# Two output rows share one middle-tap product in a dilated 3x3 convolution, with deeper f32 prefetch and two-bank PSUM tiles

## The chip, the cores and the metric

The kernel runs on one core of one Trainium2 chip; nothing else runs on the chip. The metric is the device time of one execution in microseconds (us). The *span* that a profile shows runs from the first to the last instruction and is about 2 us shorter than the time. All kernels here were timed in several rounds beside the kernel before. A difference under 2% counts as the same.

## The reference

A 3x3 convolution with dilation 2 and padding 2, f32 in and out:

```python
batch, c_in, h, w, c_out, k, dilation = 16, 64, 64, 64, 128, 3, 2
x_pad = np.pad(x, ((0, 0), (0, 0), (2, 2), (2, 2)))
output[b, co] += weight[co, ci, kh, kw] * x_pad[b, ci, kh*2 : kh*2+h, kw*2 : kw*2+w]   # summed over ci, kh, kw
```

The input is 16.8 MB, the output 33.6 MB. An output row r needs the input rows r-2, r and r+2, so rows of one parity of a pair never mix with the other parity.

## The kernel before

Two images share the 128 partitions (64 input channels each). Each is multiplied by its own 64-row half of the TensorE array, so the matmuls of the two images run side by side. A tile is 8 rows of one image: nine matmuls of up to 512 columns, one for each tap (one of the nine weights of the 3x3 window), are summed in one bank of PSUM, the memory into which TensorE writes here. Then the bank is copied to SBUF, from which DMA stores it.

```python
x32pool = ctx.enter_context(tc.tile_pool(name="x32pool", bufs=2))     # a whole pair of images, f32
cpool = ctx.enter_context(tc.tile_pool(name="cpsum", bufs=8, space=bass.MemoryType.PSUM))
# ... zero-padded f16 rows of 68 columns, weights transposed by TensorE: cut ...
def conv_matmul(x3, ps, ti, t, hb, first, last):
    dh, dw = taps[t]
    # ... rows clipped at the image's edge: cut ...
    rhs = x3[hb * CI : (hb + 1) * CI, lo + dh : hi + dh, pad + dw : pad + dw + W]
    nc.tensor.matmul(out=po, lhsT=lhsT, rhs=rhs, start=first, stop=last)

for pb in range(npairs):                      # 8 pairs of images
    for ti in range(ntiles):                  # 8 tiles of 8 rows
        for t in range(ntaps):                # 9 taps
            for hb in range(2):
                conv_matmul(x3, ps, ti, t, hb, t == 0, t == ntaps - 1)
        # ... loads and f32 -> f16 casts of the next pair: cut ...
        nc.vector.tensor_copy(out=o_sb0[:, sl], in_=ps[0])    # the engines swap on odd tiles
        nc.scalar.copy(out=o_sb1[:, sl], in_=ps[1])
        # stores of 1 MB, in the last pair of 256 KB after each tile: cut
```

## Time and profile before

| | before |
|---|---|
| time, median of 4 runs beside the change | 142.72 us (142.18 to 143.32) |
| span of the profiled run | 140.7 us |
| TensorE busy | 125.1 us |
| first to last convolution matmul | 10.6 to 134.2 us, no gap |
| bytes moved | 50.66 MB |
| DMA rate from 30 to 80 us | 423 GB/s |

Two limits lie within 3% of each other. The page of the kernel before gives, first, the busy time of each engine with its share of the span, then the span in 40 slices of 3.5 us: a digit is the busy share in tenths, and the last line is the rate of DMA. PE stands for TensorE's matmuls, PEld for its weight loads, DVE for VectorE, ACT for ScalarE, POOL for GpSimd and SP for SyncE; L133 is line 133 of the kernel.

```profile
PE 125.1 (89%) x1170; PEld 71.5 (51%) x1170; DVE 55.7 (40%) x85; ACT 53.8 (38%) x86; POOL 21.4 (15%) x49
...
PE   0049999999999999999999999999999999999910
...
DMA  4999999999999999999999999892929385799970
GB/s 97 296 415 418 415 401 414 344 428 418 424 422 422 428 417 425 429 411 424 425 424 423 422 421 428 354 414 121 426 100 431 165 356 245 298 395 402 388 307 8
```

Counted from 0, TensorE's row is full from slice 3 to slice 37. DMA's row is full only from slice 1 to slice 24, and from then on it has holes. The table by stages of the same kernel shows this in numbers. Its columns are: the stretch in us and its length, then for each engine the busy us and the number of instructions, the granted clock, the busy share of DMA and its rate.

```profile
core 0: us, PE busy (x) PEld busy (x) DVE busy (x) ACT busy (x) POOL busy (x), PEclk, DMA share, GB/s
0.00:5.00 5.00, 0.00 (x0) 0.00 (x0) 0.40 (x1) 1.28 (x1) 2.31 (x13) 1.00 0.57 136
...
30.00:80.00 50.00, 50.00 (x476) 28.58 (x473) 22.46 (x33) 20.58 (x33) 6.32 (x12) 1.00 1.02 423
...
90.00:100.00 10.00, 10.00 (x96) 5.61 (x93) 3.46 (x5) 3.09 (x6) 1.36 (x3) 1.00 0.74 308
100.00:110.00 10.00, 10.00 (x99) 5.80 (x96) 4.15 (x6) 3.35 (x6) 1.05 (x2) 1.00 0.75 312
110.00:120.00 10.00, 10.00 (x100) 5.77 (x96) 3.46 (x5) 2.93 (x6) 1.37 (x3) 1.00 0.56 229
...
125.00:135.00 10.00, 9.15 (x87) 4.94 (x81) 3.60 (x6) 3.15 (x6) 2.78 (x6) 1.00 0.98 382
135.00:140.70 5.70, 0.00 (x0) 0.00 (x0) 0.00 (x0) 0.00 (x0) 0.46 (x1) 0.63 0.30 119
```

From 30 to 80 us DMA moves 423 GB/s with a busy share of 1.02, so it is saturated; all 50.66 MB at that rate are 120 us. From 90 to 120 us the rate falls to 229 to 312 GB/s. All loads are done by then, and stores come only as fast as TensorE makes output. TensorE is busy in all of these stretches. So DMA has slack, and TensorE sets the end. The timeline of TensorE near the end gives its pace (start, duration, instruction):

```profile
128.14 0.38 PE L133 MATMUL ps_1593<-x_sb_81,w_sb 64*128 64x512 f16 x1
128.33 0.38 PE L133 MATMUL ps_1594<-x_sb_81,w_sb 64*128 64x512 f16 x1
...
130.08 0.38 PE L133 MATMUL ps_1617<-x_sb_81,w_sb 64*128 64x512 f16 x1
```

The first matmul of one tile is at 128.14 us, that of the next at 130.08: 1.94 us for nine pairs of matmuls, 0.216 us a pair. (A matmul's own 0.38 us is longer because matmuls overlap: the first two lines start 0.19 us apart.) The costs of the other engines come from the groups of instructions, one line for one shape; the columns at the end are busy us and mean ns:

```profile
L181 DVE COPY o_sb_708<-ps_829 128x512 f32<-128x512 f32 x1 | 0.7, 692 | 1.4 <-PE ps_829 L133 1.4
```

```profile
L102 ACT CAST x_sb_84<-x_964 128x1024 f16<-128x1024 f32 x1 | 1.0, 1045 | 0.9 <-PE ps_614 L133 0.9
...
L178 ACT COPY o_sb_132<-ps_134 128x512 f32<-128x512 f32 x1 | 0.6, 585 | 0.2 <-PE ps_134 L133 0.2
```

A copy of 512 columns out of PSUM takes VectorE 0.692 us and ScalarE 0.585 us, and a cast of 1024 columns takes ScalarE 1.045 us.

### The profile page before, as it was taken

What the parts mean: (1) busy time and instruction counts of PE and PEld (TensorE: products, weight loads), DVE (VectorE), ACT (ScalarE), POOL (GpSimd) and SP (SyncE); (2) the same over time, 40 slices, a digit from 0 to 9 for tenths busy, and PEclk for the clock granted to TensorE, in tenths of its full rate; (3) what the DMA queues carried; (4) which work ended last, traced back from release to release, by engine and by line L of the source; (5) the groups of instructions that cost most, each with busy time, mean ns of one, the idle gap of its engine ahead of it and who ended that gap; (6) DMA issues with size and microseconds to landing.
All of it is one profiled execution on the core that took longest, in us unless ns stands there. A gap on an engine that the chain in (4) does not pass through costs nothing.

```text
span 140.7 us, 2777 instructions
## 1 busy us (share of the span) xinstructions
PE 125.1 (89%) x1170; PEld 71.5 (51%) x1170; DVE 55.7 (40%) x85; ACT 53.8 (38%) x86; POOL 21.4 (15%) x49
## 2 busy tenths in 40 slices
PE   0049999999999999999999999999999999999910
PEld 0035555655555555655565555555565556555500
DVE  0134556535353534445353435333233333323310
ACT  3144465652535343533635253532233333322310
POOL 6000003020202020201102030202020110433210
PEclk9999999999999999999999999999999999999985
DMA  4999999999999999999999999892929385799970
GB/s 97 296 415 418 415 401 414 344 428 418 424 422 422 428 417 425 429 411 424 425 424 423 422 421 428 354 414 121 426 100 431 165 356 245 298 395 402 388 307 8
DMA packets 10733, 50.66 MB, mean 360 GB/s; under 512 B 1248, under 2 KB 1376, under 8 KB 7136
## 3 DMA queue, kind: packets, MB, share of 16 engines
q0 software_dynamic: 4816, 31.61, 54.3%
q1 hardware_dynamic: 5904, 18.88, 34.6%
q8 instruction: 9, 0.15, 0.4%
q14 instruction: 4, 0.03, 0.1%
HBM read 17.07 MB, written 33.55 MB: 360 GB/s over the span
## 4 chain that ended last, share of the span: by engine, by line
PE 73%; issue 12%; DMA 5%; POOL 3%; SPq 1%; ACT 1%; POOLq 0%
DMA x_87<-in_x_dram 5%; POOL out_dram L185 3%; PE ps_134 L133 1%; PE ps_1378 L133 1%; PE ps_1327 L133 1%; PE ps_1235 L133 1%; PE ps_1163 L133 1%; PE ps_1114 L133 1%; PE ps_1020 L133 1%; PE ps_972 L133 1%; PE ps_923 L133 1%; PE ps_829 L133 1%; PE ps_781 L133 1%; PE ps_732 L133 1%; PE ps_638 L133 1%
## 5 line engine op out<-in xcount | busy, mean ns | idle before, releaser
L133 PEld LDWEIGHTS <-w_sb 64*128 64x128 f16 x1152 | 70.2, 94 | 53.1 <-issue 1.1
L113 PE MATMUL wt_95<-ident,w_70 128*64 128x128 f16 x1 | 0.4, 377 | 7.7 <-DMA w_70<-in_weight_dram 7.7
L185 POOL DMA_DIRECT2D out_dram<-o_sb_1471 x8 | 4.3, 541 | 10.4 <-DVE o_sb_1471 L177 5.3
L100 DVE CAST x_sb_78<-x_87 128x640 f16<-128x640 f32 (+2 forms) x3 | 1.8, 606 | 8.9 <-DMA x_87<-in_x_dram 8.9
L113 PEld LDWEIGHTS <-w_70 128*64 128x64 f16 x9 | 1.1, 209 | 7.7 <-DMA w_70<-in_weight_dram 7.7
L185 POOL DMA_DIRECT2D out_dram<-o_sb_131 x2 | 1.1, 548 | 23.1 <-ACT o_sb_131 L180 19.3
L102 ACT CAST x_sb_78<-x_87 128x512 f16<-128x512 f32 (+1 forms) x2 | 1.7, 830 | 6.4 <-DMA x_87<-in_x_dram 6.4
L133 PE MATMUL ps_133<-x_sb_78,w_sb 64*128 64x512 f16 (+1 forms) x9 | 3.4, 557 | 0.0
L133 PE MATMUL ps_134<-x_sb_78,w_sb 64*128 64x512 f16 (+1 forms) x9 | 3.2, 528 | 0.0
L185 POOL DMA_DIRECT2D out_dram<-o_sb_898 x2 | 1.1, 532 | 13.1 <-ACT o_sb_898 L180 13.1
L185 POOL DMA_DIRECT2D out_dram<-o_sb_516 x2 | 1.1, 531 | 13.1 <-ACT o_sb_516 L180 13.1
L185 POOL DMA_DIRECT2D out_dram<-o_sb_707 x2 | 1.1, 531 | 13.1 <-ACT o_sb_707 L180 13.1
L185 POOL DMA_DIRECT2D out_dram<-o_sb_1089 x2 | 1.1, 531 | 13.1 <-ACT o_sb_1089 L180 13.1
L185 POOL DMA_DIRECT2D out_dram<-o_sb_325 x2 | 1.1, 531 | 13.1 <-DVE o_sb_326 L181 13.1
L185 POOL DMA_DIRECT2D out_dram<-o_sb_1280 x2 | 1.1, 531 | 12.8 <-ACT o_sb_1280 L180 12.8
L102 ACT CAST x_sb_84<-x_391 128x1024 f16<-128x1024 f32 (+1 forms) x2 | 2.0, 992 | 2.6 <-DMA x_391<-in_x_dram 2.6
L102 ACT CAST x_sb_81<-x_200 128x1024 f16<-128x1024 f32 (+1 forms) x2 | 2.0, 990 | 2.6 <-DMA x_200<-in_x_dram 2.6
L102 ACT CAST x_sb_78<-x_582 128x1024 f16<-128x1024 f32 (+1 forms) x2 | 2.0, 994 | 1.4 <-PE ps_255 L133 1.4
L100 DVE CAST x_sb_84<-x_391 128x1152 f16<-128x1152 f32 (+1 forms) x2 | 1.5, 727 | 2.4 <-DMA x_391<-in_x_dram 2.4
L102 ACT CAST x_sb_81<-x_773 128x1024 f16<-128x1024 f32 (+1 forms) x2 | 2.0, 993 | 0.9 <-PE ps_423 L133 0.9
L102 ACT CAST x_sb_78<-x_1155 128x1024 f16<-128x1024 f32 (+1 forms) x2 | 2.0, 994 | 0.9 <-PE ps_805 L133 0.9
L102 ACT CAST x_sb_81<-x_1346 128x1024 f16<-128x1024 f32 (+1 forms) x2 | 2.0, 994 | 0.9 <-PE ps_996 L133 0.9
(309 smaller groups left out, 373.2 us busy)
## 6 DMA issues: line engine op xcount, KB each, us to landing
out_dram<-o_sb_131 POOLq DMA_DIRECT2D x2, 1024.0 KB, 10.3
out_dram<-o_sb_132 POOLq DMA_DIRECT2D x2, 1024.0 KB, 13.0
out_dram<-o_sb_325 POOLq DMA_DIRECT2D x2, 1024.0 KB, 11.1
out_dram<-o_sb_326 POOLq DMA_DIRECT2D x2, 1024.0 KB, 14.3
out_dram<-o_sb_516 POOLq DMA_DIRECT2D x2, 1024.0 KB, 11.1
out_dram<-o_sb_517 POOLq DMA_DIRECT2D x2, 1024.0 KB, 14.4
out_dram<-o_sb_707 POOLq DMA_DIRECT2D x2, 1024.0 KB, 10.8
out_dram<-o_sb_708 POOLq DMA_DIRECT2D x2, 1024.0 KB, 13.4
```

Source lines behind the costliest of these rows:

```text
L100: nc.vector.tensor_copy(out=x3[:, lo:hi, pad : pad + W], in_=x32[:, lo:hi, :])
L102: nc.scalar.copy(out=x3[:, lo:hi, pad : pad + W], in_=x32[:, lo:hi, :])
L113: nc.tensor.matmul(out=wt_ps[0:CI, 0:CO], lhsT=w_slice, rhs=ident)
L133: nc.tensor.matmul(out=po, lhsT=lhsT, rhs=rhs, start=first, stop=last)
L185: nc.gpsimd.dma_start(out=out_img[2 * pb, :, e0:e1], in_=o_sb0[:, e0:e1])
```

## The change

The intent is to take matmuls off TensorE. Take two output rows of one parity, r and r+2. With w0, w1, w2 the weights of the three rows of taps, and x the input rows:

- row r is w0 x[r-2] + w1 x[r] + w2 x[r+2]
- row r+2 is w0 x[r] + w1 x[r+2] + w2 x[r+4]

Let P = w1 (x[r] + x[r+2]). Then row r = P + (w2-w1) x[r+2] + w0 x[r-2], and row r+2 = P + (w0-w1) x[r] + w2 x[r+4]. That is five products for two rows instead of six. The price: a row sum of the input on VectorE, a copy of P out of PSUM on ScalarE, and two additions of P on VectorE in place of two plain copies. A group is now 16 rows of two images, 1024 output columns for each of P, A (the even blocks) and B (the odd ones).

```diff
-    x32pool = ctx.enter_context(tc.tile_pool(name="x32pool", bufs=2))       # whole pairs
-    cpool = ctx.enter_context(tc.tile_pool(name="cpsum", bufs=8, space=bass.MemoryType.PSUM))
+    LOOK = 6
+    XB = 8
+    x32pool = ctx.enter_context(tc.tile_pool(name="x32pool", bufs=XB))      # quarters of a pair
+    xpool = ctx.enter_context(tc.tile_pool(name="xpool", bufs=3))
+    ppool = ctx.enter_context(tc.tile_pool(name="ppool", bufs=1, space=bass.MemoryType.PSUM))
+    apool = ctx.enter_context(tc.tile_pool(name="apool", bufs=3, space=bass.MemoryType.PSUM))
     # ... weights now loaded as f32 on ScalarE's queue, w2-w1 and w0-w1 formed on VectorE: cut ...
+    def product(ps, src, kind, blk0, nblk, first, last):
+        for j in (1, 0, 2):                                  # middle column first: it covers all 64
+            dw = (j - 1) * d
+            o0, o1 = max(0, -dw), W - max(0, dw)             # clipped columns: 62 of 64 for j = 0, 2
+            # ... for hb in range(2): one matmul: cut ...
     for G in range(ngroups):                                 # 32 groups
         # ... tiles, views and z (1 at an image's edge, else 0): cut ...
+        product(psP, sv, 0, 0, NBLK, True, True)
+        product(psA, blocks(x16, b0, NBLK, 1), 1, 0, NBLK, True, False)
+        product(psA, blocks(x16, b0 + z - 1, NBLK - z, 1), 2, z, NBLK - z, False, True)
+        product(psB, blocks(x16, b0, NBLK, 0), 3, 0, NBLK, True, False)
+        product(psB, blocks(x16, b0 + 1, NBLK - z, 0), 4, 0, NBLK - z, False, True)
+        nc.scalar.copy(out=p_sb, in_=psP)
+        for e, ps in ((0, psA), (1, psB)):
+            nc.vector.tensor_tensor(out=o[:, :, b0 : b0 + NBLK, e], in0=ps..., in1=pv, op=add)
+        c = G + LAG                                          # LAG = LOOK
+        if c < ngroups:
+            cast(c)
+            rowsum(c)
+            if c + XB < ngroups:
+                load(c + XB)
     # ... two stores of 1 MB from GpSimd's queue after every second group: cut ...
```

The framework's scheduler decides the order of the instructions on each engine from these dependencies; it need not be the order of the source.

More of the change, by code (lines that the diff above doesn't have):

```diff
@@ L22 @@
     CO, CI_w, KH, KW = weight.shape
-    assert CI == CI_w
-    d = 2 if isinstance(dilation, bass.AP) else int(dilation)
-    assert KH == KW == 3
-    assert CI == 64 and CO == 128
+    assert CI == CI_w == 64 and CO == 128
+    assert KH == KW == 3 and H == W == 64
     assert B % 2 == 0
+    assert not isinstance(dilation, bass.AP) and int(dilation) == 2
+    d = 2
     P = 128
-    pad = d
-    WP = W + 2 * pad
-    HW = H * W
     f32 = mybir.dt.float32
     f16 = mybir.dt.float16
-    ROWS = 512 // W
@@ L38 @@
-    ntiles = H // ROWS
-    assert H % ROWS == 0
-    NB = ROWS * W
-    CR = 2 * ROWS
-    nchunks = ntiles // 2
-    chunk_rows = [(0, CR + d)]
-    for c in range(1, nchunks - 1):
-        chunk_rows.append((c * CR + d, (c + 1) * CR + d))
-    chunk_rows.append(((nchunks - 1) * CR + d, H))
-    assert nchunks == 4
-    chunk_rows0 = [(0, ROWS + d), (ROWS + d, CR + d)] + chunk_rows[1:]
-    taps = [(0, 0)]
-    for kh in range(KH):
-        for kw in range(KW):
-            dh = (kh - KH // 2) * d
-            dw = (kw - KW // 2) * d
-            if (dh, dw) != (0, 0):
-                taps.append((dh, dw))
@@ L58 @@
-    ntaps = len(taps)
+    add = mybir.AluOpType.add
+    sub = mybir.AluOpType.subtract
+    HW = H * W
+    GR = 16
+    NG = H // GR
+    NBLK = GR // 4
+    NH = GR // 2 * W
     npairs = B // 2
-    NXB = 3
+    ngroups = npairs * NG
+    chunk_rows = [(g * GR + (d if g else 0), min((g + 1) * GR + d, H)) for g in range(NG)]
+    LOOK = 6
+    XB = 8
     wpool = ctx.enter_context(tc.tile_pool(name="wpool", bufs=1))
-    x32pool = ctx.enter_context(tc.tile_pool(name="x32pool", bufs=2))
-    xpool = ctx.enter_context(tc.tile_pool(name="xpool", bufs=1))
@@ L66 @@
-    opool = ctx.enter_context(tc.tile_pool(name="opool", bufs=4))
-    cpool = ctx.enter_context(tc.tile_pool(name="cpsum", bufs=8, space=bass.MemoryType.PSUM))
-    w16 = wpool.tile([CO, CI * KH * KW], f16, name="w16")
-    nc.gpsimd.dma_start(out=w16, in_=weight.rearrange("o i h w -> o (i h w)"))
-    ident = wpool.tile([P, P], f16, name="ident")
-    make_identity(nc, ident)
-    w_sb = wpool.tile([P, ntaps * CO], f16, name="w_sb")
-    x3_bufs = []
-    for i in range(NXB):
-        x_sb = xpool.tile([P, H * WP], f16, tag=f"xsb{i}", name=f"x_sb{i}")
-        x3 = x_sb.rearrange("p (h w) -> p h w", w=WP)
-        nc.gpsimd.memset(x3[:, :, 0:pad], 0.0)
-        nc.gpsimd.memset(x3[:, :, pad + W :], 0.0)
-        x3_bufs.append(x3)
+    x32pool = ctx.enter_context(tc.tile_pool(name="x32pool", bufs=XB))
@@ L85 @@
+    xpool = ctx.enter_context(tc.tile_pool(name="xpool", bufs=3))
+    opool = ctx.enter_context(tc.tile_pool(name="opool", bufs=3))
+    spool = ctx.enter_context(tc.tile_pool(name="spool", bufs=3))
+    ppool = ctx.enter_context(tc.tile_pool(name="ppool", bufs=1, space=bass.MemoryType.PSUM))
+    apool = ctx.enter_context(tc.tile_pool(name="apool", bufs=3, space=bass.MemoryType.PSUM))
     x_pair = x.rearrange("(nb two) c h w -> nb (two c) h w", two=2)
@@ L88 @@
     x32_tiles = {}
-    def emit_input_dma(pb):
-        x32 = x32pool.tile([P, H, W], f32, tag="x32")
-        x32_tiles[pb] = x32
-        for lo, hi in (chunk_rows0 if pb == 0 else chunk_rows):
-            nc.sync.dma_start(out=x32[:, lo:hi], in_=x_pair[pb, :, lo:hi])
-    def emit_cast(pb, lo, hi, engine):
-        x3 = x3_bufs[pb % NXB]
-        x32 = x32_tiles[pb]
-        if engine == "v":
-            nc.vector.tensor_copy(out=x3[:, lo:hi, pad : pad + W], in_=x32[:, lo:hi, :])
-        else:
-            nc.scalar.copy(out=x3[:, lo:hi, pad : pad + W], in_=x32[:, lo:hi, :])
@@ L104 @@
-    emit_input_dma(0)
-    emit_cast(0, chunk_rows0[0][0], chunk_rows0[0][1], "v")
-    emit_cast(0, chunk_rows0[1][0], chunk_rows0[1][1], "s")
-    for t, (dh, dw) in enumerate(taps):
-        kh = dh // d + KH // 2
-        kw = dw // d + KW // 2
-        w_slice = w16.rearrange("o (i k) -> o i k", k=KH * KW)[:, :, kh * KW + kw]
-        wt_ps = cpool.tile([CO, NB], f32, tag="ps", name=f"wt{t}")
-        nc.tensor.matmul(out=wt_ps[0:CI, 0:CO], lhsT=w_slice, rhs=ident)
-        nc.tensor.matmul(out=wt_ps[CI : 2 * CI, 0:CO], lhsT=w_slice, rhs=ident)
-        dst = w_sb[:, t * CO : (t + 1) * CO]
-        if t % 2 == 0:
-            nc.scalar.copy(out=dst, in_=wt_ps[:, 0:CO])
-        else:
-            nc.vector.tensor_copy(out=dst, in_=wt_ps[:, 0:CO])
@@ L121, in conv_matmul @@
-    def conv_matmul(x3, ps, ti, t, hb, first, last):
-        dh, dw = taps[t]
-        r0 = ti * ROWS
-        lo = max(r0, -dh)
-        hi = min(r0 + ROWS, H - dh)
-        lhsT = w_sb[hb * CI : (hb + 1) * CI, t * CO : (t + 1) * CO]
-        rhs = x3[
-            hb * CI : (hb + 1) * CI,
-            lo + dh : hi + dh,
-            pad + dw : pad + dw + W,
-        ]
-        po = ps[hb][:, (lo - r0) * W : (hi - r0) * W]
-        nc.tensor.matmul(out=po, lhsT=lhsT, rhs=rhs, start=first, stop=last)
@@ L135 @@
-    for pb in range(npairs):
-        x3 = x3_bufs[pb % NXB]
-        o_sb0 = opool.tile([P, HW], f32, tag="osb")
-        o_sb1 = opool.tile([P, HW], f32, tag="osb")
-        first_pair = pb == 0
-        last_pair = pb == npairs - 1
-        if last_pair:
-            flush_after = {ti: (ti * NB, (ti + 1) * NB) for ti in range(ntiles)}
-        else:
-            flush_after = {
-                ntiles // 2 - 1: (0, HW // 2),
-                ntiles - 1: (HW // 2, HW),
-            }
-        for ti in range(ntiles):
-            ps = [
-                cpool.tile([CO, NB], f32, tag="ps", name=f"ps{hb}") for hb in range(2)
-            ]
-            for t in range(ntaps):
-                for hb in range(2):
-                    conv_matmul(x3, ps, ti, t, hb, t == 0, t == ntaps - 1)
-            if first_pair:
-                if ti == 0:
-                    emit_cast(0, chunk_rows[1][0], chunk_rows[1][1], "v")
-                    emit_cast(0, chunk_rows[2][0], chunk_rows[2][1], "s")
-                elif ti == 1:
-                    emit_cast(0, chunk_rows[3][0], chunk_rows[3][1], "v")
-            if pb + 1 < npairs:
-                if ti == 2:
-                    emit_input_dma(pb + 1)
-                elif ti == 4:
-                    emit_cast(pb + 1, chunk_rows[0][0], chunk_rows[0][1], "v")
-                    emit_cast(pb + 1, chunk_rows[1][0], chunk_rows[1][1], "s")
-                elif ti == 5:
-                    emit_cast(pb + 1, chunk_rows[2][0], chunk_rows[2][1], "v")
-                    emit_cast(pb + 1, chunk_rows[3][0], chunk_rows[3][1], "s")
-            sl = slice(ti * NB, (ti + 1) * NB)
-            if ti % 2 == 0:
-                nc.vector.tensor_copy(out=o_sb0[:, sl], in_=ps[0])
-                nc.scalar.copy(out=o_sb1[:, sl], in_=ps[1])
-            else:
-                nc.scalar.copy(out=o_sb0[:, sl], in_=ps[0])
-                nc.vector.tensor_copy(out=o_sb1[:, sl], in_=ps[1])
-            if ti in flush_after:
-                e0, e1 = flush_after[ti]
-                nc.gpsimd.dma_start(out=out_img[2 * pb, :, e0:e1], in_=o_sb0[:, e0:e1])
-                if last_pair:
-                    nc.sync.dma_start(
-                        out=out_img[2 * pb + 1, :, e0:e1], in_=o_sb1[:, e0:e1]
-                    )
-                else:
-                    nc.gpsimd.dma_start(
-                        out=out_img[2 * pb + 1, :, e0:e1], in_=o_sb1[:, e0:e1]
-                    )
@@ new lines, with load, cast @@
+    x16_tiles = {}
+    xs_tiles = {}
+    def load(c):
+        pb, g = divmod(c, NG)
+        lo, hi = chunk_rows[g]
+        t = x32pool.tile([P, (GR + d) * W], f32, tag="x32", name="x32")
+        x32_tiles[c] = t
+        nc.sync.dma_start(
+            out=t[:, 0 : (hi - lo) * W].rearrange("p (h w) -> p h w", w=W),
+            in_=x_pair[pb, :, lo:hi],
+        )
+    def cast(c):
+        pb, g = divmod(c, NG)
+        lo, hi = chunk_rows[g]
+        if g == 0:
+            x16_tiles[pb] = xpool.tile([P, HW], f16, tag="x16", name="x16")
+            xs_tiles[pb] = xpool.tile([P, HW // 2], f16, tag="xs", name="xs")
+        nc.scalar.copy(
+            out=x16_tiles[pb][:, lo * W : hi * W], in_=x32_tiles.pop(c)[:, 0 : (hi - lo) * W]
+        )
@@ new lines, in rowsum @@
+    def rowsum(c):
+        pb, g = divmod(c, NG)
+        v = x16_tiles[pb][:, g * GR * W : (g + 1) * GR * W].rearrange(
+            "p (b e q) -> p b e q", e=2, q=2 * W
+        )
+        s = xs_tiles[pb][:, g * NH : (g + 1) * NH].rearrange("p (b q) -> p b q", q=2 * W)
+        nc.vector.tensor_tensor(out=s, in0=v[:, :, 0], in1=v[:, :, 1], op=add)
+    w32 = wpool.tile([CO, CI * KH * KW], f32, name="w32")
+    nc.scalar.dma_start(out=w32, in_=weight.rearrange("o i h w -> o (i h w)"))
+    for c in range(XB):
+        if c < ngroups:
+            load(c)
@@ new lines @@
+    ident = wpool.tile([P, P], f16, name="ident")
+    make_identity(nc, ident)
+    KINDS = 5
+    wd = wpool.tile([CO, KINDS * KW * 2 * CI], f16, name="wd")
+    wdv = wd.rearrange("o (k j r i) -> o k j r i", k=KINDS, j=KW, r=2)
+    wv = w32.rearrange("o (i h w) -> o h w i", h=KH, w=KW)
+    for r in range(2):
+        nc.vector.tensor_copy(out=wdv[:, 0, :, r], in_=wv[:, 1])
+        nc.vector.tensor_tensor(out=wdv[:, 1, :, r], in0=wv[:, 2], in1=wv[:, 1], op=sub)
+        nc.vector.tensor_tensor(out=wdv[:, 3, :, r], in0=wv[:, 0], in1=wv[:, 1], op=sub)
+        nc.scalar.copy(out=wdv[:, 2, :, r], in_=wv[:, 0])
+        nc.scalar.copy(out=wdv[:, 4, :, r], in_=wv[:, 2])
@@ new lines @@
+    w_sb = wpool.tile([P, KINDS * KW * CO], f16, name="w_sb")
+    NT = KINDS * KW
+    for q in range(0, NT, 8):
+        n = min(8, NT - q)
+        wt = apool.tile([P, 1024], f32, tag="ab", name="wt")
+        for t in range(q, q + n):
+            nc.tensor.matmul(
+                out=wt[:, (t - q) * CO : (t - q + 1) * CO],
+                lhsT=wd[:, t * 2 * CI : (t + 1) * 2 * CI],
+                rhs=ident,
+            )
+        h = n // 2 * CO
+        nc.vector.tensor_copy(out=w_sb[:, q * CO : q * CO + h], in_=wt[:, 0:h])
+        nc.scalar.copy(out=w_sb[:, q * CO + h : (q + n) * CO], in_=wt[:, h : n * CO])
@@ new lines, in product @@
+    def product(ps, src, kind, blk0, nblk, first, last):
+        for j in (1, 0, 2):
+            dw = (j - 1) * d
+            o0, o1 = max(0, -dw), W - max(0, dw)
+            t = kind * KW + j
+            for hb in range(2):
+                pp = slice(hb * CI, (hb + 1) * CI)
+                rhs = src(pp, dw + o0, dw + o1)
+                po = ps[:, hb * NH + blk0 * 2 * W : hb * NH + (blk0 + nblk) * 2 * W]
+                po = po.rearrange("p (r w) -> p r w", w=W)[:, :, o0:o1]
+                nc.tensor.matmul(
+                    out=po,
+                    lhsT=w_sb[pp, t * CO : (t + 1) * CO],
+                    rhs=rhs,
+                    start=first and j == 1,
+                    stop=last and j == 2,
+                )
@@ new lines, in blocks @@
+    def blocks(x16, b0, n, e):
+        v = x16.rearrange("p (b e r w) -> p b e r w", e=2, r=2, w=W)
+        return lambda pp, c0, c1: v[pp, b0 : b0 + n, e, :, c0:c1]
+    LAG = LOOK
+    for c in range(min(LAG, ngroups)):
+        cast(c)
+        rowsum(c)
+        if c + XB < ngroups:
+            load(c + XB)
+    o_tiles = {}
+    for G in range(ngroups):
+        pb, g = divmod(G, NG)
+        x16 = x16_tiles[pb]
+        xs = xs_tiles[pb].rearrange("p (r w) -> p r w", w=W)
+        if g == 0:
+            o_tiles[pb] = opool.tile([P, 2 * HW], f32, tag="osb", name="osb")
+        o = o_tiles[pb].rearrange("p (m b e q) -> p m b e q", m=2, e=2, q=2 * W)
+        b0 = g * NBLK
+        psP = ppool.tile([P, 2 * NH], f32, tag="p", name="psP")
+        sv = lambda pp, c0, c1: xs[pp, g * GR // 2 : (g + 1) * GR // 2, c0:c1]
+        product(psP, sv, 0, 0, NBLK, True, True)
+        psA = apool.tile([P, 2 * NH], f32, tag="ab", name="psA")
+        product(psA, blocks(x16, b0, NBLK, 1), 1, 0, NBLK, True, False)
+        z = 1 if g == 0 else 0
+        product(psA, blocks(x16, b0 + z - 1, NBLK - z, 1), 2, z, NBLK - z, False, True)
+        psB = apool.tile([P, 2 * NH], f32, tag="ab", name="psB")
+        product(psB, blocks(x16, b0, NBLK, 0), 3, 0, NBLK, True, False)
+        z = 1 if g == NG - 1 else 0
+        product(psB, blocks(x16, b0 + 1, NBLK - z, 0), 4, 0, NBLK - z, False, True)
+        p_sb = spool.tile([P, 2 * NH], f32, tag="psb", name="p_sb")
+        nc.scalar.copy(out=p_sb, in_=psP)
+        pv = p_sb.rearrange("p (m b q) -> p m b q", m=2, q=2 * W)
+        for e, ps in ((0, psA), (1, psB)):
+            nc.vector.tensor_tensor(
+                out=o[:, :, b0 : b0 + NBLK, e],
+                in0=ps.rearrange("p (m b q) -> p m b q", m=2, q=2 * W),
+                in1=pv,
+                op=add,
+            )
+        c = G + LAG
+        if c < ngroups:
+            cast(c)
+            rowsum(c)
+            if c + XB < ngroups:
+                load(c + XB)
+        if g % 2 == 1:
+            e0, e1 = (g - 1) * GR * W, (g + 1) * GR * W
+            for m in range(2):
+                nc.gpsimd.dma_start(
+                    out=out_img[2 * pb + m, :, e0:e1],
+                    in_=o_tiles[pb][:, m * HW + e0 : m * HW + e1],
+                )
```

## The prediction

> What bounds the kernel now. Two limits lie close together. TensorE: the page shows it 89% busy, and the timeline shows it without a gap from 10.6 us (first convolution matmul) to 134.2 us: 123.6 us of a 140.7 us span. A tile of 9 taps takes 1.94 us: 0.216 us for a pair of 512-column matmuls, one for each image, running side by side. DMA: in the table by stages it moves 423 GB/s from 30 to 80 us with a busy share of 1.02, so it is saturated too; from 90 to 120 us it falls to 229-312 GB/s, because the loads are done and the stores wait for TensorE. All 50.66 MB at 423 GB/s are 120 us. The Trainium skill, "DMA: Bandwidth & Descriptors", section Specifications, gives a fabric ceiling of 435 GB/s; the trace's 423 agrees, so I expect no higher plateau.
>
> What the change does. TensorE: per 16 output rows of two images, 15 pairs of matmuls (5 products of 3 taps) instead of 18; two taps of three write 62 columns of 64. Estimate: 5 x 0.216 + 10 x 0.209 = 3.17 us a group, 32 groups, minus 2.5 us for clipped edge rows: 99 us instead of 122. Evictions before: 128 copies of 512 columns (VectorE 0.692 us, ScalarE 0.585 us). After, a group has on ScalarE one copy of 1024 columns from PSUM (estimate 0.585 + 512 x 0.83 ns = 1.01 us) and one cast of 1024 (1.045 us in the trace): 66 us in all. VectorE has two adds of 1024 columns from PSUM (estimate 0.692 + 512 x 1.04 ns = 1.23 us each) and one f16 row sum of 512 (0.42 us if two elements a cycle, as the Trainium skill, "VectorE: DVE Perf Modes", section on the perf-mode tier table, has it for 16-bit tensor_tensor in SBUF; no run here shows it yet): 2.9 us a group, 92 us in all, within 10% of TensorE. Bytes do not change.
>
> On the critical path. The 23 us taken from TensorE cannot all be had: a group moves 1.57 MB, 3.7 us at 423 GB/s, more than TensorE's 3.1 or VectorE's 2.9. The kernel turns DMA-bound. TensorE starts at about 10 to 11 us as before and ends near 112 us; stores drain after that. The deep prefetch (8 load buffers plus 6 casts ahead: 7.6 MB, 18 us of traffic) fills the time before the first store, about 21 us, so DMA stays full from about 2.3 us on. Sum: 2.3 start + 120 traffic + about 1 of lost feeding + 3.6 from the last bytes to the end of the span (137.1 to 140.7 before) = 127 us of span; the time is 2 us above the span before, so 129 us.
>
> Predicted 129 us, 126 to 134 eight times in ten. Faster by over 2%: 0.93; within 2%: 0.05; slower: 0.02.
>
> What would show it. DMA near 420 GB/s from 4 us to the last slices; TensorE busy about 100 us and ending 8 to 12 us before the last store lands; stores taking 10 us or more to land in the second half; VectorE about 92 us; ScalarE about 70 us.
>
> What would make it wrong. VectorE adds slower than estimated: it sets the pace at 3.2 us or more, and a late finish leaves the last stores exposed (132 to 136). The single PSUM buffer of the shared product, if its ScalarE copy queues behind a cast that waits for a load. A scheduler order that delays the first groups, so that DMA idles near 15-22 us. Write-only traffic slower than mixed traffic.

## The result and the profile after

| | before | after |
|---|---|---|
| time, median of 4 runs | 142.72 us | 130.80 us (130.71 to 131.05) |
| span of the profiled run | 140.7 us | 128.8 us |
| TensorE, VectorE, ScalarE busy | 125.1, 55.7, 53.8 us | 104.1, 90.0, 66.0 us |
| convolution on TensorE | 10.6 to 134.2 us | 12.1 to 114.8 us |
| bytes moved | 50.66 MB | 50.76 MB |

The ratio of the times is 0.9176, with a 95% interval of 0.9137 to 0.9214. Ratios in this document are the mean time of one kernel's runs over that of the kernel before in the same rounds, so not quite the ratio of the medians quoted. Executions over 1.5% slower than the fastest of the same kernel are left out of the means.

The page of the kernel after, same lines as before:

```profile
PE 104.1 (81%) x975; PEld 55.7 (43%) x975; DVE 90.0 (70%) x104; ACT 66.0 (51%) x71; POOL 17.8 (14%) x38
...
PE   0052999999999999999999999999999999960000
...
DMA  3999999999999999999999999999999999999930
GB/s 87 354 412 404 419 411 410 405 422 424 425 429 412 427 425 419 415 426 423 418 420 422 426 426 423 425 428 425 422 425 428 425 422 425 428 425 420 433 150 5
```

The two rows have changed places. DMA is now full from slice 1 to slice 37, and TensorE stops in slice 35. The table by stages of the kernel after, same columns:

```profile
core 0: us, PE busy (x) PEld busy (x) DVE busy (x) ACT busy (x) POOL busy (x), PEclk, DMA share, GB/s
0.00:5.00 5.00, 0.00 (x0) 0.00 (x0) 0.00 (x0) 1.28 (x1) 0.70 (x6) 1.00 0.56 167
5.00:10.00 5.00, 1.87 (x15) 1.44 (x15) 2.74 (x7) 3.79 (x7) 0.00 (x0) 1.00 1.02 406
10.00:30.00 20.00, 17.80 (x152) 8.57 (x154) 15.05 (x24) 17.31 (x21) 2.22 (x4) 1.00 1.03 414
30.00:80.00 50.00, 49.75 (x478) 27.03 (x479) 42.97 (x48) 30.41 (x32) 8.41 (x17) 1.00 1.02 422
...
90.00:100.00 10.00, 10.00 (x99) 5.43 (x96) 8.02 (x8) 3.04 (x3) 2.11 (x4) 1.00 1.01 425
100.00:110.00 10.00, 10.00 (x101) 5.55 (x98) 7.85 (x7) 3.75 (x4) 1.06 (x2) 1.00 1.01 423
110.00:120.00 10.00, 4.75 (x48) 2.38 (x42) 4.78 (x4) 1.31 (x2) 2.11 (x4) 0.95 1.01 427
120.00:125.00 5.00, 0.00 (x0) 0.00 (x0) 0.00 (x0) 0.00 (x0) 0.00 (x0) 0.50 0.70 295
125.00:128.80 3.80, 0.00 (x0) 0.00 (x0) 0.00 (x0) 0.00 (x0) 0.00 (x0) 0.50 0.02 6
```

The rate stays at 422 to 427 GB/s from 30 to 120 us, where the kernel before had fallen to 229. The last addition ends at 116.1 us, and DMA still works for 10 us after it. The groups of instructions of the kernel after show the new work (the first number after the bar is busy us, the second the mean ns of one, then the idle time ahead of it with what ended most of it):

```profile
L191 ACT COPY p_sb<-psP 128x1024 f32<-128x1024 f32 x32 | 32.4, 1012 | 35.6 <-PE psP L146 27.1
L194 DVE TENSOR_TENSOR osb<-psA,p_sb 128x1024 f32<-128x1024 f32 x32 | 39.1, 1220 | 11.3 <-PE psA L146 8.8
L194 DVE TENSOR_TENSOR osb<-psB,p_sb 128x1024 f32<-128x1024 f32 x32 | 38.9, 1217 | 0.0
```

The timelines of VectorE, TensorE and GpSimd of the kernel after give the row sum, the first and the last product and the first store:

```profile
9.13 0.42 DVE L98 TENSOR_TENSOR xs<-x_132 128x512 f16<-128x512 f16 x1 [0.61 <-ACT x_132 L88]
```

```profile
12.11 1.43 PE L146 MATMUL psP<-xs,w_sb 64*128 64x512 f16 x6 [2.48 <-DVE w_sb L132]
...
113.46 1.29 PE L146 MATMUL psB<-x_1129,w_sb 64*128 64x512 f16 x12
```

```profile
24.47 1.20 POOL L211 DMA_DIRECT2D out_dram<-osb  x2 [23.16 <-DVE osb L194]
```

The row sum of 512 f16 elements takes 0.42 us. The last product starts at 113.46 us. The first store goes out at 24.47 us. DMA had moved about 8.9 MB by then (0.84 + 2.03 MB in the first two stretches of the table, and 14.5 us at 414 GB/s), so it never ran dry. The landing times of stores, from the page's list of DMA issues, were 10 to 14 us for the early 1 MB stores before and have a median of 14.6 us after.

One detail at the end matters below. The trace holds 16 landing records for each of these transfers; they are read here as one for each of the core's 16 DMA engines. For the last store of the kernel after, the first record is at 122.96 us of the span, the 15th at 125.06 and the last at 126.64, a spread of 3.7 us. In the kernel before, the last store's spread is 1.0 us. The table by stages shows the same as a fading rate: 295 GB/s from 120 to 125 us, with a share of 0.70.

### The profile page after: what moved, and what is told of

Same layout as the page of the kernel before. It is cut to its first block, busy times and chain, and to the rows that moved or that the text cites. A ratio compares the mean times of both kernels' runs of the same rounds, so it can differ in the third digit from the quotient of the medians.

```text
span 128.8 us, 2360 instructions
## 1 busy us (share of the span) xinstructions
PE 104.1 (81%) x975; PEld 55.7 (43%) x975; DVE 90.0 (70%) x104; ACT 66.0 (51%) x71; POOL 17.8 (14%) x38
## 2 busy tenths in 40 slices
DMA packets 9369, 50.76 MB, mean 394 GB/s; under 512 B 1040, under 2 KB 1040, under 8 KB 5264
## 5 line engine op out<-in xcount | busy, mean ns | idle before, releaser
L146 PEld LDWEIGHTS <-w_sb 64*128 64x128 f16 x960 | 54.2, 95 | 50.8 <-issue 4.3
L191 ACT COPY p_sb<-psP 128x1024 f32<-128x1024 f32 x32 | 32.4, 1012 | 35.6 <-PE psP L146 27.1
L194 DVE TENSOR_TENSOR osb<-psA,p_sb 128x1024 f32<-128x1024 f32 x32 | 39.1, 1220 | 11.3 <-PE psA L146 8.8
L194 DVE TENSOR_TENSOR osb<-psB,p_sb 128x1024 f32<-128x1024 f32 x32 | 38.9, 1217 | 0.0
L211 POOL DMA_DIRECT2D out_dram<-osb x32 | 17.1, 537 | 99.1 <-DVE osb L194 99.1
L146 PE MATMUL psP<-xs,w_sb 64*128 64x496 f16 (+1 forms) x192 | 26.6, 379 | 2.9 <-DVE w_sb L132 2.5
L126 PE MATMUL wt<-ident,wd 128*128 128x128 f16 x15 | 1.9, 311 | 7.8 <-DVE wd L115 7.8
L146 PE MATMUL psA<-x_132,w_sb 64*128 64x496 f16 (+3 forms) x48 | 6.7, 421 | 0.0
L146 PE MATMUL psB<-x_132,w_sb 64*128 64x496 f16 (+3 forms) x48 | 6.1, 390 | 0.0
L146 PE MATMUL psA<-x_150,w_sb 64*128 64x496 f16 (+3 forms) x48 | 5.6, 365 | 0.0
L146 PE MATMUL psB<-x_453,w_sb 64*128 64x496 f16 (+3 forms) x48 | 5.6, 365 | 0.0
L146 PE MATMUL psB<-x_150,w_sb 64*128 64x496 f16 (+3 forms) x48 | 5.6, 365 | 0.0
L146 PE MATMUL psB<-x_282,w_sb 64*128 64x496 f16 (+3 forms) x48 | 5.6, 365 | 0.0
L146 PE MATMUL psA<-x_453,w_sb 64*128 64x496 f16 (+3 forms) x48 | 5.6, 365 | 0.0
L146 PE MATMUL psB<-x_795,w_sb 64*128 64x496 f16 (+3 forms) x48 | 5.6, 365 | 0.0
L146 PE MATMUL psB<-x_624,w_sb 64*128 64x496 f16 (+3 forms) x48 | 5.6, 365 | 0.0
L146 PE MATMUL psA<-x_966,w_sb 64*128 64x496 f16 (+3 forms) x48 | 5.6, 365 | 0.0
L146 PE MATMUL psB<-x_966,w_sb 64*128 64x496 f16 (+3 forms) x48 | 5.6, 365 | 0.0
L146 PE MATMUL psB<-x_1129,w_sb 64*128 64x496 f16 (+3 forms) x48 | 5.6, 365 | 0.0
L146 PE MATMUL psA<-x_282,w_sb 64*128 64x496 f16 (+3 forms) x48 | 5.6, 365 | 0.0
L146 PE MATMUL psA<-x_624,w_sb 64*128 64x496 f16 (+3 forms) x48 | 5.6, 365 | 0.0
L146 PE MATMUL psA<-x_795,w_sb 64*128 64x496 f16 (+3 forms) x48 | 5.6, 365 | 0.0
## 6 DMA issues: line engine op xcount, KB each, us to landing
out_dram<-osb POOLq DMA_DIRECT2D x32, 1024.0 KB, 14.6
x_628<-in_x_dram SPq DMA_DIRECT2D x1, 576.0 KB, 14.5
```

Of the source, the lines that this page charges most:

```text
L126: nc.tensor.matmul(out=wt[:, (t - q) * CO : (t - q + 1) * CO], lhsT=wd[:, t * 2 * CI : (t + 1) * 2 * CI], rhs=ident,)
L146: nc.tensor.matmul(out=po, lhsT=w_sb[pp, t * CO : (t + 1) * CO], rhs=rhs, start=first and j == 1, stop=last and j == 2,)
L191: nc.scalar.copy(out=p_sb, in_=psP)
L194: nc.vector.tensor_tensor(out=o[:, :, b0 : b0 + NBLK, e], in0=ps.rearrange("p (m b q) -> p m b q", m=2, q=2 * W), in1=pv, op=add,)
L211: nc.gpsimd.dma_start(out=out_img[2 * pb + m, :, e0:e1], in_=o_tiles[pb][:, m * HW + e0 : m * HW + e1],)
```

## The experiments

Beside the change itself, twelve kernels were run. "Wrong" means that a kernel computes something else in order to take away a cost.

| run | what it is | median, us | ratio to before |
|---|---|---|---|
| after | the change | 130.80 | 0.918 |
| less_pe | 9 pairs of matmuls a group for 15 (wrong) | 129.68 | 0.908 |
| half_stores | every second image not stored (wrong) | 124.22 | 0.870 |
| six_products | the change without the shared product | 144.88 | 1.014 |
| stores_sp | stores from SyncE's queue | 133.55 | 0.935 |
| shallow | 2 load buffers, 2 casts ahead | 184.48 | 1.294 |
| before_deep | kernel before, 4 load buffers for 2 | 143.32 | 1.003 |
| wide | no clipped columns (wrong) | 130.98 | 0.918 |
| tail_15 | last store in parts of 120 and 8 partitions | 131.31 | 0.920 |
| look2 | 8 load buffers, 2 casts ahead | 130.96 | 0.917 |
| xb2 | 2 load buffers, 6 casts ahead | 184.61 | 1.294 |
| late_sp | half of the late stores from SyncE | 130.75 | 0.916 |
| xb4 | 4 load buffers | 143.09 | 1.003 |

The kernel before had medians of 142.46 to 142.90 us beside them.

### less_pe: is TensorE off the critical path?

```diff
-        product(psA, blocks(x16, b0, NBLK, 1), 1, 0, NBLK, True, False)
-        product(psA, blocks(x16, b0 + z - 1, NBLK - z, 1), 2, z, NBLK - z, False, True)
+        product(psA, blocks(x16, b0, NBLK, 1), 1, 0, NBLK, True, True)
         # the same for psB: product 4 is left out
```

> Wrong result on purpose: the products with the outer taps of the block before and after are left out, so a group has 9 pairs of matmuls instead of 15 and TensorE loses about 40 us of work. Theory (DMA bounds the changed kernel from about 5 us on): 129 to 131 us, no faster by over 1%, DMA still near 423 GB/s to the end. Rival (compute still sets the pace, the full DMA is a coincidence): VectorE's 2.9 us a group takes over and the time falls to 122 us or less.

It took 129.68 us, 1.1 us or 0.9% less than the change, inside the expected range. Three lines of the table by stages of this kernel (same columns):

```profile
30.00:110.00 80.00, 59.69 (x468) 28.15 (x467) 67.45 (x72) 41.54 (x42) 13.69 (x26) 0.91 1.01 424
110.00:120.00 10.00, 0.00 (x0) 0.00 (x0) 1.00 (x1) 0.00 (x0) 1.05 (x2) 0.62 1.01 428
120.00:125.00 5.00, 0.00 (x0) 0.00 (x0) 0.00 (x0) 0.00 (x0) 0.00 (x0) 0.50 0.64 269
```

TensorE has 59.7 us of work between 30 and 110 us instead of about 80, and DMA's rate is the same: 424 GB/s, in the change 423. So taking 40% of the matmuls away buys almost nothing: TensorE does not set the time of the changed kernel. The 1.0 us of span that did go lies in the landing of the last store, 125.67 us instead of 126.64.

### half_stores: how far off is the next limit?

```diff
-            for m in range(2):
+            for m in range(1):
                 nc.gpsimd.dma_start(
```

> Wrong result on purpose: the second image of each pair is computed but never stored, 16.8 MB of 50.8 MB less to move (40 us of DMA at 423 GB/s). Theory: the time falls to what TensorE and VectorE leave: TensorE ends near 114 us, then one add, one store of 1 MB and the closing, 121 to 125 us. So the second limit stands only 6 to 9 us below the first. Rival (compute or its waits bound the kernel already): 129 us or more.

It took 124.22 us, inside the expected range. Two lines of its table by stages:

```profile
90.00:110.00 20.00, 20.00 (x198) 11.02 (x196) 16.03 (x14) 6.38 (x7) 1.59 (x3) 1.00 0.41 166
110.00:120.00 10.00, 5.17 (x52) 2.60 (x46) 5.02 (x5) 1.72 (x2) 1.06 (x2) 0.99 0.48 197
```

DMA is at 166 GB/s there, and TensorE has no gap. With a third less traffic the kernel is bound by compute again, and that limit is 6.6 us below the measured time of the change. So both runs agree: DMA bounds the change, and compute stands close behind.

### six_products: which part of the change pays?

```diff
-        product(psP, sv, 0, 0, NBLK, True, True)
-        product(psA, blocks(x16, b0, NBLK, 1), 1, 0, NBLK, True, False)
+        product(psA, blocks(x16, b0, NBLK, 0), 0, 0, NBLK, True, False)
+        product(psA, blocks(x16, b0, NBLK, 1), 2, 0, NBLK, False, False)
         # ... psB alike; three kinds of weights for five; no row sum ...
-        nc.scalar.copy(out=p_sb, in_=psP)
-        # two additions on VectorE
+        # psA copied by ScalarE, psB by VectorE
```

> All of the change but the shared product: six products for two rows, summed in PSUM, no row sum, no addition afterwards; clipped columns, deep prefetch, 2-bank tiles and order are kept. Right result. Theory (the shared product is what pays): TensorE needs 3.80 us a group, about 119 us, ends near 132 us, and the last 2 MB of stores stand behind it: 140 to 145 us, the gain over the kernel before is gone. Rival (prefetch and clipping bring most of the gain): 134 us or less.

It is correct and took 144.88 us, 1.4% slower than the kernel before (the same, by the 2%). Its TensorE timeline ends with the first line; GpSimd's ends with the second, for two stores of 1 MB:

```profile
130.31 1.91 PE L143 MATMUL psB<-x,w_sb 64*128 64x512 f16 x18
```

```profile
134.04 1.05 POOL L198 DMA_DIRECT2D out_dram<-osb  x2 [6.40 <-issue]
```

TensorE works until 132.2 us, 1.9 us earlier than before. But its last two stores are 1 MB each, where the kernel before stored 256 KB after each tile; the last byte lands 8.5 us after the last matmul (140.68 us), before 4.2 us (138.39 against 134.2). So on their own, clipping, prefetch, larger tiles and order do not gain; with them in place, the shared product is worth 14.1 us (144.88 to 130.80).

### before_deep and wide: prefetch by itself, and the change without its clipping

```diff
-    x32pool = ctx.enter_context(tc.tile_pool(name="x32pool", bufs=2))
+    x32pool = ctx.enter_context(tc.tile_pool(name="x32pool", bufs=4))
```

> The kernel before with four f32 load buffers instead of two, nothing else. Theory (it is bound by TensorE from 10.6 to 134.2 us without a gap, and loads that come earlier free nothing): 142 to 144 us, within 1%. Rival (the prefetch is worth time by itself): below 140 us.

It took 143.32 us, ratio 1.003: no gain. The loads were all issued by 54 us, and TensorE's work still had no gap.

```diff
-            o0, o1 = max(0, -dw), W - max(0, dw)
+            o0, o1 = 0, W
-                rhs = src(pp, dw + o0, dw + o1)
+                rhs = src(pp, 0, W)
```

> Wrong result on purpose: every tap reads and writes all 64 columns unshifted, so the clipping of columns is undone in TensorE's time (10 of 15 matmul pairs go from 496 to 512 columns, about 2.1 us in all). Theory: DMA bounds, TensorE ends at about 117 instead of 115 us, 130.4 to 131.2 us, no change. Rival (TensorE's chain still counts): 132 to 133 us.

It took 130.98 us. TensorE's last product starts at 115.38 us instead of 113.46, and the last store lands at 126.67 us instead of 126.64. The clipping's 1.9 us or so are real on TensorE and worth nothing to the time. (In the trace of wide ScalarE also runs one cast and one copy of P, near the start, in the other order.)

### shallow, look2, xb2 and xb4: what the deep prefetch is worth

```diff
-    LOOK = 6
-    XB = 8
+    LOOK = 2
+    XB = 2
```

> Prefetch cut from 8 load buffers and 6 casts ahead to 2 and 2, nothing else. Theory (the deep prefetch pays by giving DMA work before the first store): only about 3.5 MB are moved by the first store at about 20 us, where the changed kernel had moved 6.9 MB, so some 8 us of DMA time are lost and the time is 137 to 143 us; TensorE's start hardly moves. Rival (the prefetch is a convenience, the loads would come in time anyway): 130 to 132 us.

It took 184.48 us. The direction was right and the size was not: the loss is 54 us, not 8. The waits of this kernel (who waited for what: us in total, times, longest us):

```profile
ACT x L88 <- DMA x<-in_x_dram: 51.2, 19, 6.8
PE psP L146 <- ACT p_sb L191: 41.2, 9, 6.3
```

A cast whose load has not landed stands at the head of ScalarE's queue, and the copy of the shared product out of its single PSUM buffer stands behind the cast. The timeline of ScalarE in shallow shows one such case. The P that the second line copies was complete at 69.1 us; the copy came 7.8 us later, right behind the cast:

```profile
75.99 0.94 ACT L88 CAST x<-x 128x896 f16<-128x896 f32 x1 [4.47 <-DMA x<-in_x_dram]
76.83 1.00 ACT L191 COPY p_sb<-psP 128x1024 f32<-128x1024 f32 x1
```

TensorE then waits for that copy before it may write the next P: after these two lines its next product starts at 77.89 us, with 6.29 us of idle time ahead of it. This is the second danger that the prediction named, now switched on.

The next two runs were meant to part the number of load buffers from the distance of the casts.

```diff
-    LOOK = 6      # look2: XB stays 8
+    LOOK = 2
-    XB = 8        # xb2: LOOK stays 6
+    XB = 2
```

> Undoes half of the shallow run: 8 load buffers again, but still only 2 casts ahead. The shallow run came out at 184 us instead of the 137 to 143 expected; its trace shows ScalarE waiting 51 us for loads and TensorE 41 us for ScalarE's copy of the shared product. Theory (a cast at the head of ScalarE's in-order queue that waits for a load holds up the copy behind it; only the number of loads in flight counts): casts find their loads landed, 130.5 to 134 us. Rival (it is the distance of the casts ahead of the matmuls that counts): 150 us or more.

> The other half: 2 load buffers, 6 casts ahead. Theory (as in look2): the 6 groups of casts in hand do not help, since ScalarE stands still at a cast whose load is late whatever has been cast before, and the copy of the shared product stands behind it: 160 to 190 us. Rival (the distance of the casts counts): 142 us or less.

look2 took 130.96 us and xb2 184.61. Both fit the theory, but for a weaker reason than it seemed. A listing of the compiled instructions, engine by engine, showed look2 to be the same program as the change, and xb2 the same as shallow: the scheduler draws every cast forward as far as the three cast buffers allow, whatever LOOK says. The two runs are repeats (within 0.2 us) and say nothing about casts ahead. What they leave is the number of load buffers. With 2 of them the traces also show another order of casts, additions and row sums in places, so shallow is not the effect of the buffers alone; the next run is.

```diff
-    XB = 8
+    XB = 4
```

> 4 load buffers. Listing the instructions showed that the number of casts ahead in the source is dead: with it at 2 or 6 the scheduler puts out the same order on every engine, so look2 repeated the changed kernel and xb2 repeated shallow. What is left of the explanation of shallow is the number of loads in flight: the scheduler puts ScalarE's casts in bunches of four, one for each quarter of a pair; with two buffers the third and fourth can only be issued after the first two casts and each costs a round trip of about 5 us with ScalarE's queue standing still, about 6.3 us a pair. This run keeps the changed kernel's order to the letter and only has 4 buffers. Theory (a whole bunch in flight is enough): no wait of ScalarE for loads past the first 20 us, and only the start is poorer in traffic, 131 to 136 us. Rival (each cast exposes its load's round trip until the buffers cover more than a bunch): 145 us or more.

It took 143.09 us (141.98 to 144.84), between the two expectations, so neither theory had the size. The order of instructions is that of the change, so this is the pure effect of four load buffers fewer. The profiled run took 144.84 us and counts as slow (2.0% above the fastest of the other three, which took 141.98 to 143.12); its table by stages serves only to show where the traffic is missing:

```profile
5.00:10.00 5.00, 1.87 (x15) 1.44 (x15) 2.73 (x7) 3.75 (x7) 0.00 (x0) 1.00 0.79 313
10.00:30.00 20.00, 14.68 (x112) 6.41 (x114) 11.67 (x19) 15.04 (x17) 1.20 (x2) 1.00 0.87 293
...
90.00:120.00 30.00, 26.86 (x246) 13.66 (x244) 20.95 (x21) 11.98 (x12) 4.22 (x8) 0.94 0.86 356
```

From 10 to 30 us DMA moves 293 GB/s instead of 414; with 20 us at 121 GB/s less, 2.4 MB or 5.7 us are lost (1.1 us more between 5 and 10 us). The waits of the same run show that loads are late beyond the start as well (the longest wait of a cast, 2.5 us, is at 51.7 us):

```profile
ACT x L88 <- DMA x<-in_x_dram: 14.7, 12, 2.5
PE psP L146 <- ACT p_sb L191: 12.1, 6, 3.5
```

So a bunch of four casts in flight is not enough. A 512 KB load had a median of 4.3 us to landing in shallow, where DMA was often idle, and 9.0 us in xb4, where it was mostly full: in the fuller system each load takes longer, so more of them must be under way. How the 12 us divide exactly between the poor start and the later waits was not tested.

### stores_sp, late_sp and tail_15: the uneven end

These three ask why the last store's landing records spread over 3.7 us.

```diff
-                nc.gpsimd.dma_start(
+                nc.sync.dma_start(
```

> The stores are issued from SyncE's queue instead of GpSimd's, nothing else. In the changed kernel the 16 landing records of the last store are spread over 3.7 us, one of them 1.6 us behind all others, while DMA's rate fades from 369 to 25 GB/s over the last 4 us. Theory (one of the 16 DMA engines is slowed by the descriptors that GpSimd writes, as the Trainium skill guesses in DMA: Bandwidth & Descriptors, section Latency and other measured facts): the spread falls below 2.2 us and the time by 1 to 2 us, to 129 to 130. Rival (the engines drift apart whoever issues): the spread stays over 3 us and the time within 0.5 us of 130.8.

It took 133.55 us, slower than the change. The spread is 3.8 us (127.02 to 130.80), so the theory fell (its rival had the spread right, but not the time), though the single straggler is gone: the 15th record is at 130.60, 0.2 us ahead of the last. The time went elsewhere. Waits of SyncE's queue in this kernel:

```profile
SPq L211 <- DVE osb L194: 30.2, 8, 5.9
SPq L211 <- DMA out_dram<-osb: 22.2, 11, 2.8
...
SPq L77 <- DMA x<-in_x_dram: 8.6, 9, 1.7
```

Loads and stores now stand in one queue, in order, and wait for each other and for earlier landings; DMA fell to 344 GB/s from 20 to 40 us.

```diff
+                q = nc.sync if m == 1 and pb >= 5 else nc.gpsimd
-                nc.gpsimd.dma_start(
+                q.dma_start(
```

> Right result; try for a better version. From the sixth pair of images on, when no load is left to issue, the second image's stores go through SyncE's queue and the first's through GpSimd's. In the changed kernel the last DMA engine lands 1.6 us after the 15th, and with all stores from SyncE that single laggard was gone, though that kernel lost time because loads and stores waited for one another in one queue. Theory (GpSimd's path makes one engine lag): the gap between the 15th and the last landing falls below 0.8 us and the time to 129.3 to 130.3 us. Rival (the drift is the engines' own): 130.6 us or more.

It took 130.75 us, the change's time within 0.1 us. The records of the transfer that landed last are at 122.84, 124.82 (15th) and 126.83 us: the gap is still 2.0 us. The rival holds as far as this goes. But the store that landed last is one from GpSimd; the last one from SyncE, 1.8 us earlier, has a gap of 1.4 us, so this run does not clear GpSimd's path.

```diff
+                if G == ngroups - 1 and m == 1:       # all other stores as before: cut
+                    for p0, p1 in ((0, 120), (120, 128)):
+                        nc.sync.dma_start(out=out_img[2 * pb + m, p0:p1, e0:e1], in_=o_tiles[pb][p0:p1, ...])
```

> Right result. The very last store of 1 MB is issued from SyncE in two parts, partitions 0 to 119 and 120 to 127, which 128 does not force onto all 16 DMA engines alike: 120 partitions divide over 15 engines and 8 over 8. In the changed kernel one of the 16 landing records of each late store comes 1.6 us after the other 15. Theory (one DMA engine lags steadily, and it is the one that 15-way and 8-way transfers leave out): the late record disappears from the last landing, the end comes 0.8 to 1.5 us earlier, 129.3 to 130.1 us. Rival (the laggard is another engine, or another one each time): 130.6 us or more, lag unchanged.

The reading that 120 partitions use 15 engines and 8 use 8 is from the Trainium skill, "DMA: Bandwidth & Descriptors", section on why a DMA increments its semaphore by 16. The records of this run agree: for the part of 120 partitions one record stands alone at 116.66 us, as its issue ended, and 15 follow from 120.67 to 124.77 us; for the part of 8, one at 117.86 us and 8 from 121.94 to 126.13 us.

The run took 131.31 us, so the theory's time failed. What landed last is not the split store but the other image's, issued by GpSimd over all 128 partitions: its records begin at 121.47 us, the 15th is at 126.54 and the last at 126.92. None of the last three transfers has a straggler (gaps ahead of the last record of 0.3, 0.4 and 0.4 us), and still the end did not come earlier. As far as the records tell, the slow engine was not left out: the store before had its last record at 123.56 us, in the change at 121.75. From 119.3 us on, the last record of one more store and then everything to the end took 7.65 us, in the change 7.34. This fits a slow engine that has a share in both parts of the split store (estimate: 64 KB for each of three stores in the change, 8 KB more here, 7.34 x 200/192 = 7.65), which is the rival's "another engine". The records do not name their engines, so this is argued and not shown. Why the other engines ended 1.5 us later than in the change stays open too.

The landing records of several kernels, in us of the span, for the transfer that landed last:

| kernel | first | 15th | last | DMA |
|---|---|---|---|---|
| before | 137.39 | 137.59 | 138.39 | nearly full from 125 us on, gaps before |
| after | 122.96 | 125.06 | 126.64 | full to the end |
| wide | 124.85 | 124.98 | 126.67 | a hole from 118 to 120 us |
| less_pe | 122.79 | 124.88 | 125.67 | full to the end |
| stores_sp | 127.02 | 130.60 | 130.80 | full to the end |
| half_stores | 120.74 | 120.91 | 120.94 | with gaps |
| six_products | 140.58 | 140.66 | 140.68 | with gaps |

Where DMA had gaps near the end (half_stores, six_products), all records lie within 0.2 us. Where it was full from start to end, they lie 2.9 to 4.0 us apart (with late_sp). In wide the last two stores were issued 1.9 us later than in the change, DMA fell to 213 and then 311 GB/s between 118 and 120 us, and 15 records came within 0.13 us of each other; yet the last came at 126.67 us, as in the change. So that hole cost nothing: at the very end the slowest engine alone sets the time.

The drift is not made at the end. In the change, the records of a store that landed at 83.4 us lie 2.4 us apart, and those of one at 116.9 us 3.9 us. The kernel before drifted as well: 3.0 us for the store that landed at 92.2 us. Then its DMA began to have gaps, and at 101.0 us the spread was 0.2 us. So gaps let the engines draw level. They are not the whole story: between stores with a spread of 0.2 us, one record of a store in the kernel before came 1.9 us behind the other 15 (at 105.3 us), and of another 1.3 us (at 118.2 us). What makes an engine slower was not found.

## Why the prediction was right

**DMA takes over as the bound: shown.** DMA ran at 422 to 427 GB/s from 30 to 120 us; less_pe changed 0.9%, half_stores gave 124 us. The fear that traffic of stores alone would be slower did not come true: the last load landed at 81.0 us, and the rate after it was 423 to 427 GB/s.

**The 23 us of TensorE cannot all be had: shown.** TensorE's convolution shrank from 123.6 us (10.6 to 134.2) to 102.7 us (12.1 to 114.8), 21 us, and the time by 11.9 us. TensorE needed a little more than the 99 us predicted and ended at 114.8 instead of 112 us, which cost nothing: in wide it ended 1.9 us later still, and the kernel's time was the same to within 0.2 us.

**Costs on the other engines: right.** VectorE's additions took 1.22 us (estimate 1.23), ScalarE's copy 1.01 (1.01), the row sum 0.42 (0.42). VectorE was busy 90.0 us (92) and ScalarE 66.0 (66). The prediction does not say where its 0.83 and 1.04 ns a column come from; the trace before has copies of 128 columns out of PSUM at 0.27 us (ScalarE) and 0.283 us (VectorE), which with the copies of 512 give 0.82 and 1.07 ns.

**No higher plateau than 423 GB/s: right.** The 435 GB/s of the page on DMA was not reached over any of the long stretches.

**The prefetch fills the time before the first store: right in effect, wrong in its details.** The prediction counted 8 load buffers plus 6 casts, 7.6 MB, and the first store at 21 us. The number 6 is dead in this program: SyncE had issued 20 loads, 8 + 12 (three cast buffers of four), before the first store, and this store came at 24.5 us, because ScalarE worked through those casts ahead of the first copies of P. DMA had enough to do all the same, so the lateness cost nothing. That depth is needed was only half seen: xb4 and shallow show that without it not merely the start suffers but the whole gain is lost.

**The sum was 127 us of span and 128.8 was measured.** The term that was mis-sized is "3.6 from the last bytes to the end of the span". The parts measured: by 30 us, 11.1 MB had moved, 26.3 us of traffic, so 3.7 us were lost (2.3 + 1 predicted); 50.76 MB at 423 GB/s are 120.0 us (120 predicted); what is left of 128.8 us is 5.1 us for the end, not 3.6. The 3.6 us came from the kernel before, as 1.3 us for the fading of the last store and 2.3 us of closing after the last landing (138.4 to 140.7). The closing hardly changed (2.1 us). The other part grew from 1.3 to about 2.9 us, and that is the drift of the DMA engines: the 16 records of the last store have a mean of 124.0 us and a maximum of 126.6. In the kernel before the drift stood at 3.0 us too, at 92 us, but its gaps let the engines draw level, so the 1.3 us read off its end were too few for a DMA that is never idle.

## What to carry to other kernels

When two limits stand 3% apart, work taken from the first pays only up to the second; add up the bytes at the measured plateau before counting on the rest. A change that moves the bound to DMA must also keep DMA fed from the first microseconds, and the buffers for that must cover the landing time of a load in a full system, not in an idle one. In shallow one cast that waited for a load held up the copy of P behind it on ScalarE, and TensorE behind that; look for such a queue. A constant in the source that is meant to set a distance may be dead under a scheduler, so compare the compiled order before reading a meaning into two runs.

## What the Trainium skill lacked or had wrong

- "DMA: Bandwidth & Descriptors", section Latency and other measured facts, says that two engines are usually slower and guesses at GpSimd's descriptor rings, for transfers issued there only. Here the last store's records spread 3.7 us with stores from GpSimd and 3.8 us with all from SyncE; only the single straggler (1.6 us behind the 15th, 0.2 us with SyncE) fits the guess.
- The same page says nothing of the engines drifting apart under unbroken load. Here: 2.9 to 4.0 us at the end of 120 us without a gap; in the kernel before 3.0 us at 92 us, and 0.2 us after its first gaps.
- The same page, section Where 436 GB/s comes from, says that HBM's limit of about 358 GB/s for a core, and not the fabric's 435, binds transfers between HBM and SBUF. This core, alone, read and wrote 422 to 427 GB/s for 90 us, 2 to 3% under the 435, so the 358 did not bind it (the same note calls a measured 425 GB/s near the fabric's rate). "HBM Reference", section Specifications, has about 425 for a lone core, which agrees.
- "VectorE: DVE Perf Modes", section on the perf-mode tier table, agrees: the f16 row sum of 512 took 0.42 us, and f32 additions with one PSUM operand took 1.22 us for 1024 columns, one element a cycle of the page's 0.96 GHz (estimate: 1.07 us) and a rest of 0.15 us. Nothing is wrong there.
- On the number of load buffers, "Trainium Kernel Development and Optimization", section Best Practices, says only to double-buffer; no page relates it to the landing time of a load. Here 2, 4 and 8 buffers of 0.5 MB gave 184.5, 143.1 and 130.8 us.
